# Attention scores in two passes over 128 lines, with queries and keys spread inside SBUF

## The chip, the core and the metric

One NeuronCore of a Trainium2 chip. The metric is the device time of the whole program in microseconds (us), median of several runs. A profile is one more execution, recorded by the hardware; its times are given as us from the start of its span. TensorE is PE in the profile, VectorE is DVE, ScalarE is ACT, GpSimd is POOL, and SyncE, which here only issues transfers, is SP. A "line" of SBUF below is one of its 128 partitions.

## The reference

One layer of a decoder trunk on 512 tokens of width 1024, in float32: an input projection, a causal pooling mixer on 512 channels beside attention on the other 512 (8 heads of 64), an output projection, a gated MLP with a short convolution, and a gated embedding. For 512 tokens in blocks of 256, the selected past blocks and the own block together are plain causal attention, with a bias by distance. What matters here is the scores of a head:

```python
l_own = jnp.einsum('bhqd,bhkd->bhqk', qc, k_own).astype(jnp.float32) * scale + bias_own
l_own = jnp.where(d_own >= 0, l_own, -jnp.inf)
probs = jax.nn.softmax(logits, axis=-1)
```

The contraction is over `d`, the 64 channels of one head.

## The kernel before

**Numbers.** Matmuls run on a 4-byte type (fp32r) that keeps fewer bits than float32. So each operand is held as a pair, a high part `hi` (ACT rounds it) and a low part `lo` (DVE subtracts), and a product is three matmuls into one bank of PSUM: lo by hi, hi by lo, hi by hi (`mm3`, L220 to L222). `split` makes a pair (L225 ACT, L226 DVE).

**Order.** The program writes out the order of each engine's instructions by hand: every engine, and every queue of transfers, takes its instructions in the order of the program text and waits at the first that is not ready. SP issues all transfers of weights.

**Weights.** `_Weights` has a list of chunks of 1 MB. Each lands in one of two buffers `raw` and is split in two steps, each into a pair `wh`, `wl` (ACT L143, DVE L144) that feeds one product. `W.ahead(n)` splits up to n pairs beyond those used. When the second step of a chunk is split, its buffer is free and the chunk after next is issued on SP (L114), which waits for the DVE instruction. In the attention stage chunk 5 is issued in the projection of query pair 0, chunk 6 in that of key pair 0, chunk 7 in the first pooling projection `pool_in(0)`. In `project` these steps come ahead of the rounding of its own result.

**Attention.** `query(hp)` and `key(hp)` project a pair of heads: 24 matmuls of 512 columns into a bank `mm`, then the high part by ACT (L408, or L225) and the low part by DVE (L409, L226), in tiles `qh`, `ql`, `kh`, `kl` with two buffers each. Lines 0 to 63 are the even head, 64 to 127 the odd one. `scores(h)` takes the four query tiles of the causal triangle (128 queries by 512, 384, 128 and 256 keys), three matmuls each on the 64 lines of the head: 12 matmuls. Then DVE adds the bias and finds the maximum (L430), ACT takes the exponential (L432), and DVE normalizes `L` (L433, L436). `transposes(h)` turns `L` into ten 128 by 128 blocks (PE L451), which are split to `PT` (L225, L226). `values(h)` is eight matmuls on `V` and `PT` (L471), low before high at each block of keys.

The loop over heads keeps PE busy with other products (`fills`) while the softmax of a head runs:

```python
    for h in range(H - 1):
        for f in fills[h]:
            f()
        transposes(h)
        scores(h + 1)
        values(h)
```

Ahead of the loop come `query(0)`, `query(1)`, `key(0)`, `key(1)`, the split of `wpool`, and `scores(0)`. `fills` holds the four pooling projections (heads 0, 1, 5, 6), query and key pairs 2 and 3 (heads 2 to 4) and two small products `pool_out` (heads 2 and 3). After the loop the output projection starts, with the transposes and values of head 7 inside it.

Of the kernel before, what the change touches and what calls it, by code (L numbers as in the profile page):

```python
# [17 lines left out]
F32 = mybir.dt.float32  # L18
F32R = mybir.dt.float32r
# [48 lines left out]
class _Weights:  # L68
# [10 lines left out]
    def cols(self, w, col):  # L79

        self.chunks.append(([w[:, col:col + 256].rearrange("(k p) c -> p k c", p=P)], 2))

    def rows(self, w, k0, n, col, width):

        src = w[k0 * P:(k0 + n) * P, col:col + width]
        self.chunks.append(([src.rearrange("(k p) c -> p k c", p=P)], 1))
# [9 lines left out]
    def load(self, between=None):  # L96
        c = self.loaded
        srcs, axis = self.chunks[c]
        self.loaded += 1
        if axis is None:  # L100
            return
        raw = self.pool.tile([P, 2048], F32, tag="raw", name=f"raw{c}", bufs=self.RAW)
        if axis == 0:
            self.raw[c] = raw.rearrange("p (s a b) -> p s a b", s=2, a=2)
            for s, src in enumerate(srcs):
                self.nc.sync.dma_start(self.raw[c][:, s, :src.shape[1], :], src)
        else:
            src = srcs[0]
            self.raw[c] = raw.rearrange("p (a b) -> p a b", a=src.shape[1])
            n = 2 if c < 2 else 1  # L110
            step = src.shape[1] // n
            for i in range(n):
                part = slice(i * step, (i + 1) * step)
                self.nc.sync.dma_start(self.raw[c][:, part, :], src[:, part, :])  # L114
                if between is not None:
                    between(i)

    def ahead(self, n):

        while self.split < min(self.used + n, 2 * len(self.chunks)):  # L120
            c, s = divmod(self.split, 2)
            while self.loaded <= c:
                self.load()
            srcs, axis = self.chunks[c]
            if axis is None:
                view = srcs[s][0]
            elif axis == 0:
                view = self.raw[c][:, s, :srcs[s].shape[1], :]
            else:
                raw = self.raw[c]  # L130
                half = raw.shape[axis] // 2
                part = slice(s * half, (s + 1) * half)
                view = raw[:, part, :] if axis == 1 else raw[:, :, part]
            pair = []
            for kind in "hl":
                t = self.pool.tile([P, 1024], F32R, tag="w" + kind, name=f"w{kind}{self.split}", bufs=self.PAIRS)
                size = view.shape[1] * view.shape[2]
                pair.append(t[:, :size].rearrange("p (a b) -> p a b", a=view.shape[1]))
            if axis is None:
                for t, src in zip(pair, srcs[s]):  # L140
                    self.nc.sync.dma_start(t.bitcast(F32), src)
            else:
                self.nc.scalar.copy(pair[0], view)  # L143
                self.nc.vector.tensor_sub(pair[1], view, pair[0].bitcast(F32))  # L144
            self.pairs[self.split] = pair
            self.split += 1
            if s == 1:
                self.raw.pop(c, None)
                while self.loaded < min(c + 1 + self.RAW, len(self.chunks)):
                    self.load()  # L150
# [8 lines left out]
def hybrid_layer(ctx, tc, x, p, rel_bias, g_mix_pre, g_mix_post, g_ffn_pre, g_ffn_post, w_in, w_pool,  # L159
# [20 lines left out]
    W.cols(w_in, 512)  # L180
    W.cols(w_in, 1024)
    W.cols(w_in, 0)
    W.cols(w_in, 768)
    W.cols(w_in, 1280)
    W.cols(w_in, 256)
    for n in range(2):
        for k0 in (0, 4):
# [36 lines left out]
    def split(pair, src):  # L224
        act.copy(pair[0], src)  # L225
        dve.tensor_sub(pair[1], src, pair[0].bitcast(F32))  # L226
# [173 lines left out]
        W.ahead(n)  # L400
        return ps

    qT, kT, L = {}, {}, {}

    def query(hp):
        ps = project(f"q{hp}")
        hi, lo = qT[hp] = [ap2.tile([P, S], F32R, tag=f"q{c}", name=f"q{c}{hp}", bufs=2) for c in "hl"]
        act.mul(hi, ps, -(DH ** -0.5))  # L408
        dve.scalar_tensor_tensor(lo, ps, -(DH ** -0.5), hi.bitcast(F32), op0=ALU.mult, op1=ALU.subtract)  # L409

    def key(hp):
        ps = project(f"k{hp}")
        kT[hp] = [ap2.tile([P, S], F32R, tag=f"k{c}", name=f"k{c}{hp}", bufs=2) for c in "hl"]
        split(kT[hp], ps)

    place = {3: (0, 0, 768), 2: (1, 0, 384), 0: (1, 384, 0), 1: (2, 0, 128)}

    def scores(h):
        hp, e = divmod(h, 2)
        rows = slice(e * DH, (e + 1) * DH)  # L420
        bk = [bank(f"s{h}_{b}", "s") for b in range(3)]
        for i, (b, c, _) in place.items():
            n = (i + 1) * P
            mm3(bk[b][:, c:c + n], [q[rows, i * P:n] for q in qT[hp]], [q[rows, :n] for q in kT[hp]], True, True)
        L[h] = ap2.tile([P, 1280], F32, tag="L", name=f"L{h}", bufs=1)
        m = small.tile([P, 12], F32, tag="m", name=f"m{h}", bufs=2)
        for i, (b, c, o) in place.items():
            n = (i + 1) * P
            l = L[h][:, o:o + n]
            dve.tensor_tensor_reduce(out=l, in0=bk[b][:, c:c + n], in1=T[:, h, S - n:], scale=1.0, scalar=MASKED,  # L430
                                     op0=ALU.add, op1=ALU.min, accum_out=m[:, i:i + 1])
            act.activation(l, l, AF.Exp, bias=m[:, i:i + 1], scale=-1.0, accum_out=m[:, 4 + i:5 + i])  # L432
        dve.reciprocal(m[:, 8:], m[:, 4:8])  # L433
        for i, (b, c, o) in place.items():
            l = L[h][:, o:o + (i + 1) * P]
            dve.tensor_scalar_mul(l, l, m[:, 8 + i:9 + i])  # L436
# [19 lines left out]
    def moving(q, j):  # L456
        if j < 3:
            o = (P, P + 512, P + 896)[j]
            return q[:, o:o + (NT - j) * P]
        return q.rearrange("p (a b) -> p a b", b=P)[:, 0::10, :]  # L460

    def values(h):
        hp, e = divmod(h, 2)
        ps = bank(f"o{h}", "pt")
        for j in range(NT):
            o = ps[:, min(j, 2) * P:]
            if j == 3:
                o = o.rearrange("p (a b) -> p a b", b=P)
            w = V[:, j, hp, e].rearrange("p a d -> p (a d)")
            for c in (1, 0):  # L470
                pe.matmul(o, w, moving(PT[c], j), start=j == 0 and c == 1, stop=j == NT - 1 and c == 0)  # L471
        rows = slice(e * DH, (e + 1) * DH)
        other = slice((1 - e) * DH, (2 - e) * DH)
        hi, lo = (q[rows, 4 + hp, :] for q in yT)
# [40 lines left out]
    def y_stationary(t, k):  # L515
# [2 lines left out]
    yb = {}  # L518
    part = (4, 5, 0, 1, 6)
    query(0)  # L520
    query(1)
    key(0)
    key(1)
    split(wp, wpool)
    scores(0)
    fills = {0: [lambda: pool_in(0)], 1: [lambda: pool_in(1)],
             2: [lambda: query(2), lambda: pool_out(0)],
             3: [lambda: query(3), lambda: key(2), lambda: pool_out(1)],
             4: [lambda: key(3)], 5: [lambda: pool_in(2)],
             6: [lambda: pool_in(3)]}  # L530
    after = {1: lambda: pool_mid(0), 2: lambda: pool_mid(1), 6: lambda: pool_mid(2)}
    for h in range(H - 1):
        for f in fills[h]:
            f()
        transposes(h)
        scores(h + 1)
        values(h)
        if h in after:
            after[h]()
# [505 lines left out]
```

## Time and profile before

| what | us |
|---|---|
| median of 3 runs | 600.74 (598.84 to 600.99) |
| the profiled execution, its own time | 602.42 |
| its span, first to last instruction | 600.7 |
| PE busy in the span | 591.5 (98%) |
| DVE busy | 429.0 (71%) |
| ACT busy | 293.0 (49%) |
| POOL busy | 235.6 (39%) |

Busy time is read as time in which the engine had an instruction running. PE's is an upper limit of its use, since the ends of matmuls are modelled. 1.7 us of the profiled execution's time lie outside its span. The attention stage runs from about 40 to 145 us: `scores(0)` starts at 61.61 us, the transposes of head 0 at 69.31 and those of head 7 at 145.72.

### The profile page before, as it was taken

What the parts mean: (1) busy time and instruction counts of PE and PEld (TensorE: products, weight loads), DVE (VectorE), ACT (ScalarE), POOL (GpSimd) and SP (SyncE); (2) the same over time, 40 slices, a digit from 0 to 9 for tenths busy, and PEclk for the clock granted to TensorE, in tenths of its full rate; (3) what the DMA queues carried; (4) which work ended last, traced back from release to release, by engine and by line L of the source; (5) the groups of instructions that cost most, each with busy time, mean ns of one, the idle gap of its engine ahead of it and who ended that gap; (6) DMA issues with size and microseconds to landing.
All of it is one profiled execution on the core that took longest, in us unless ns stands there. A gap on an engine that the chain in (4) does not pass through costs nothing.

```text
span 600.7 us, 7462 instructions
## 1 busy us (share of the span) xinstructions
PE 591.5 (98%) x2784; PEld 490.9 (82%) x2784; DVE 429.0 (71%) x556; ACT 293.0 (49%) x476; POOL 235.6 (39%) x236
## 2 busy tenths in 40 slices
PE   9999999999999999999999999999999999999995
PEld 5888888888888998888888888888888788888884
DVE  4653577778378668699855748867778786878984
ACT  5433565575445433344333514625636655765561
POOL 2300230046215559999901697584230000003920
PEclk9999999999999999999999999999999999999999
DMA  8676202122651596999962765867464576852892
GB/s 291 205 269 208 70 1 73 68 71 104 213 167 43 182 361 228 363 335 348 353 210 78 255 210 197 285 237 237 183 214 153 176 280 186 294 189 66 316 308 113
DMA packets 63373, 122.29 MB, mean 204 GB/s; under 512 B 3571, under 2 KB 32847, under 8 KB 61928
## 3 DMA queue, kind: packets, MB, share of 16 engines
q1 hardware_dynamic: 53752, 82.39, 40.8%
q0 software_dynamic: 9584, 39.41, 17.9%
q8 instruction: 22, 0.36, 0.3%
q14 instruction: 15, 0.12, 0.1%
HBM read 97.65 MB, written 26.76 MB: 207 GB/s over the span
## 4 chain that ended last, share of the span: by engine, by line
PE 92%; DVE 2%; DMA 2%; ACT 1%; issue 1%; POOL 0%; SPq 0%; POOLq 0%; DVEq 0%
PE gate L220 6%; PE valu L220 6%; PE valu L222 6%; PE gate L222 6%; PE gate L221 6%; PE valu L221 6%; PE d L220 6%; PE d L222 6%; PE d L221 6%; PE y L220 2%; PE y L221 2%; PE y L222 2%; DMA wl<-gsum 2%; PE g L221 1%; PE o L471 1%; PE g L222 1%
## 5 line engine op out<-in xcount | busy, mean ns | idle before, releaser
L144 DVE TENSOR_TENSOR wl<-raw,wh 128x1024 fp32r<-128x1024 f32 (+1 forms) x118 | 161.5, 1376 | 28.9 <-ACT wh L143 28.4
L143 ACT CAST wh<-raw 128x1024 fp32r<-128x1024 f32 (+1 forms) x118 | 118.8, 1023 | 32.6 <-DMA raw<-in_w_up 13.1
L715 POOL TENSOR_TENSOR b<-b 128x512 f32<-128x512 f32 x60 | 95.8, 1607 | 12.5 <-DMA b<-in_w_down 10.1
L220 PE MATMUL gate<-hT,wl 128*128 128x512 f32 x160 | 62.3, 389 | 0.0
L221 PE MATMUL gate<-hT,wh 128*128 128x512 f32 x160 | 62.3, 389 | 0.0
L222 PE MATMUL gate<-hT,wh 128*128 128x512 f32 x160 | 62.2, 389 | 0.0
L220 PE MATMUL valu<-hT,wl 128*128 128x512 f32 x160 | 62.2, 389 | 0.0
L221 PE MATMUL valu<-hT,wh 128*128 128x512 f32 x160 | 62.2, 389 | 0.0
L222 PE MATMUL valu<-hT,wh 128*128 128x512 f32 x160 | 62.2, 389 | 0.0
L220 PE MATMUL d<-wh,ml 128*128 128x512 f32 x154 | 60.0, 390 | 0.6 <-DVE ml L226 0.6
L222 PE MATMUL d<-wh,mh 128*128 128x512 f32 x154 | 59.9, 389 | 0.0
L221 PE MATMUL d<-wl,mh 128*128 128x512 f32 x154 | 59.9, 389 | 0.0
L250 POOL TENSOR_SCALAR rd<-msd 128x1 f32<-128x1 f32 x4 | 3.2, 798 | 107.1 <-ACT M L245 107.0
L492 POOL TENSOR_TENSOR u<-u 128x512 f32<-128x512 f32 x10 | 11.6, 1158 | 81.7 <-ACT u L488 81.3
L659 ACT ACTIVATE sq<-sq 128x512 f32<-128x512 f32 x22 | 13.9, 633 | 53.8 <-DVE sq L658 53.8
L647 ACT ACTIVATE c<-gate,cols 128x512 f32<-128x512 f32 x20 | 15.5, 773 | 46.9 <-PE gate L222 46.9
L222 PEld LDWEIGHTS gate<-hT,wh 128*128 128x128 f32 x160 | 30.0, 188 | 6.3
L222 PEld LDWEIGHTS valu<-hT,wh 128*128 128x128 f32 x160 | 30.0, 188 | 6.3
L221 PEld LDWEIGHTS valu<-hT,wh 128*128 128x128 f32 x160 | 30.0, 188 | 6.2
L220 PEld LDWEIGHTS valu<-hT,wl 128*128 128x128 f32 x160 | 30.0, 188 | 6.2
L221 PEld LDWEIGHTS gate<-hT,wh 128*128 128x128 f32 x160 | 30.0, 188 | 6.2
L220 PEld LDWEIGHTS gate<-hT,wl 128*128 128x128 f32 x160 | 30.0, 188 | 6.2
(245 smaller groups left out, 1365.0 us busy)
## 6 DMA issues: line engine op xcount, KB each, us to landing
raw<-in_w_up SPq DMA_DIRECT2D x22, 1024.0 KB, 5.3
b<-in_w_down POOLq DMA_DIRECT2D x22, 512.0 KB, 7.4
tsum<-b POOLq DMA_DIRECT2D x11, 1024.0 KB, 5.4
raw<-tsum SPq DMA_DIRECT2D x20, 512.0 KB, 5.6
raw<-in_w_down SPq DMA_DIRECT2D x15, 512.0 KB, 5.9
raw<-in_w_in SPq DMA_DIRECT2D x6, 1024.0 KB, 6.4
raw<-in_w_out SPq DMA_DIRECT2D x4, 1024.0 KB, 5.0
b<-in_w_ple_gate POOLq DMA_DIRECT2D x8, 512.0 KB, 4.6
```

The lines of the kernel that those rows point to most:

```text
L143: self.nc.scalar.copy(pair[0], view)
L144: self.nc.vector.tensor_sub(pair[1], view, pair[0].bitcast(F32))
L220: pe.matmul(o, st[1], mv[0], start=first, stop=False, skip_group_check=more)
L221: pe.matmul(o, st[0], mv[1], start=False, stop=False, skip_group_check=more)
L222: pe.matmul(o, st[0], mv[0], start=False, stop=last, skip_group_check=more)
L250: pool.tensor_scalar(r, ms, add, None, op0=ALU.add)
L471: pe.matmul(o, w, moving(PT[c], j), start=j == 0 and c == 1, stop=j == NT - 1 and c == 0)
L492: pool.tensor_tensor(out=nxt[:, 16:], in0=src[:, 16:], in1=src[:, 16 - (1 << lvl):16 + S - (1 << lvl)], op=ALU.add)
L647: act.activation(c0, pg, AF.Identity, bias=cw[:, 3, f:f + 1], scale=cw[:, 2, f:f + 1])
L659: act.activation(sq, sq, AF.Tanh, scale=GELU_A * GELU_C)
L715: pool.tensor_tensor(out=b[:, o, :], in0=b[:, i0, :], in1=b[:, i1, :], op=ALU.subtract)
```

## The change

The scores take two matmuls over all 128 lines where they took three over 64. For head e of a pair the tile `ST[e][0]` holds the head's `hi` queries on its own 64 lines and the `lo` queries on the other 64. `ST[e][1]` holds the `hi` keys on both halves, and beside them the `lo` keys on both halves. One matmul against the `lo` keys and one against the `hi` keys then sum all four products (the low by low one too, which was left out). The pair's result is first written to one tile `QK` (query high, key high, key low, query low; one buffer) and from there copied to `ST` by transfers within SBUF, issued on SP: four of 128 KB for the queries of a pair, four of 256 KB for its keys. `QK` and `ST` have one buffer each, so the next pair's query or key can be written to `QK` only when the transfers have read it, and the next pair's transfers may write `ST` only when the scores have read it.

The order of the weights is changed to match (chunks 5 and 6 each hold a query pair and a key pair in rows of 512 bytes, in two transfers, where they held two query pairs or two key pairs in rows of 1 KB), and query 3 comes behind key 2. `values` takes all its high parts first, then the low ones.

```diff
+    def two(self, w, *cols):
+        self.chunks.append(([w[:, c:c + P].rearrange("(k p) c -> p k c", p=P) for c in cols], 3))
...
-    W.cols(w_in, 768)
-    W.cols(w_in, 1280)
+    for c in (768, 896):
+        W.two(w_in, c, c + 512)
...
+    QK = ap2.tile([P, 4, S], F32R, name="qk")
+    ST = [[ap2.tile([P, S], F32R, name=f"q_{e}"), ap2.tile([P, 2, S], F32R, name=f"k_{e}")] for e in range(2)]

     def query(hp):
         ps = project(f"q{hp}")
-        hi, lo = qT[hp] = [ap2.tile([P, S], F32R, tag=f"q{c}", name=f"q{c}{hp}", bufs=2) for c in "hl"]
-        act.mul(hi, ps, -(DH ** -0.5))
-        dve.scalar_tensor_tensor(lo, ps, -(DH ** -0.5), hi.bitcast(F32), op0=ALU.mult, op1=ALU.subtract)
+        act.mul(QK[:, 0, :], ps, -(DH ** -0.5))
+        dve.scalar_tensor_tensor(QK[:, 3, :], ps, -(DH ** -0.5), QK[:, 0, :].bitcast(F32), op0=ALU.mult,
+                                 op1=ALU.subtract)

     def key(hp):
         ps = project(f"k{hp}")
-        kT[hp] = [ap2.tile([P, S], F32R, tag=f"k{c}", name=f"k{c}{hp}", bufs=2) for c in "hl"]
-        split(kT[hp], ps)
+        split([QK[:, 1, :], QK[:, 2, :]], ps)
+
+    def spread_queries():
+        for e in range(2):
+            for a in range(2):
+                sp.dma_start(ST[e][0][a * DH:(a + 1) * DH].bitcast(F32),
+                             QK[e * DH:(e + 1) * DH, 0 if a == e else 3, :].bitcast(F32))
+
+    def spread_keys():
+        for e in range(2):
+            for a in range(2):
+                sp.dma_start(ST[e][1][a * DH:(a + 1) * DH].bitcast(F32), QK[e * DH:(e + 1) * DH, 1:3, :].bitcast(F32))

     def scores(h):
-        hp, e = divmod(h, 2)
-        rows = slice(e * DH, (e + 1) * DH)
+        q, k = ST[h % 2]
...
-            mm3(bk[b][:, c:c + n], [q[rows, i * P:n] for q in qT[hp]], [q[rows, :n] for q in kT[hp]], True, True)
+            for a in (1, 0):
+                pe.matmul(bk[b][:, c:c + n], q[:, i * P:n], k[:, a, :n], start=a == 1, stop=a == 0)
...
     def values(h):
-        for j in range(NT):
...
-            for c in (1, 0):
-                pe.matmul(o, w, moving(PT[c], j), start=j == 0 and c == 1, stop=j == NT - 1 and c == 0)
+        for c in range(2):
+            for j in range(NT):
...
+                pe.matmul(o, w, moving(PT[c], j), start=j == 0 and c == 0, stop=j == NT - 1 and c == 1)
...
     query(0)
+    spread_queries()
     query(1)
     key(0)
+    spread_keys()
     key(1)
     split(wp, wpool)
     scores(0)
...
-             3: [lambda: query(3), lambda: key(2), lambda: pool_out(1)],
+             3: [lambda: key(2), spread_keys, lambda: query(3), lambda: pool_out(1)],
...
         scores(h + 1)
+        if h in (0, 2, 4):
+            spread_queries()
+            if h != 2:
+                spread_keys()
         values(h)
```

## Rows read from the trace of the kernel before

**Rows 1.** The page of the kernel before: the chain of work that ended last, by engine.

```profile
PE 92%; DVE 2%; DMA 2%; ACT 1%; issue 1%; POOL 0%; SPq 0%; POOLq 0%; DVEq 0%
```

**Rows 2.** The waits of TensorE (PE) over the whole span, the one of the attention stage: who waited <- for whom, us in total, times, longest.

```profile
PE pt L451 <- DVE L L436: 0.5, 1, 0.5
```

**Rows 3.** Timeline of PE from the transposes of head 0 to the end of the projection behind `values(0)`: start us, us, line, operation, what it writes <- reads, x how many. An instruction's own length is modelled and overlaps the next, so the pace is the distance of two starts.

```profile
69.31 1.25 PE L451 MATMUL pt<-ident,L 128*128 128x128 f32 x10
70.50 0.50 PE L220 MATMUL s<-kh,ql 64*128 64x512 f32 x1
...
71.30 0.33 PE L220 MATMUL s<-kh,ql 64*128 64x384 f32 x1
71.47 0.34 PE L221 MATMUL s<-kl,qh 64*128 64x384 f32 x1
...
71.89 0.27 PE L221 MATMUL s<-kl,qh 64*128 64x128 f32 x1
72.00 0.27 PE L222 MATMUL s<-kh,qh 64*128 64x128 f32 x1
...
72.61 1.56 PE L471 MATMUL o<-PT,V 128*128 128x512 f32 x8
74.01 0.40 PE L220 MATMUL u<-hT,wl 128*128 128x512 f32 x1
...
79.23 0.39 PE L222 MATMUL u<-hT,wh 128*128 128x512 f32 x1
```

**Rows 4.** The same view at three places without 64-line matmuls beside them: the transposes and `values` of head 7, and a run of 38 matmuls of 256 columns.

```profile
145.72 1.29 PE L451 MATMUL pt<-ident,L 128*128 128x128 f32 x10 [0.47 <-DVE L L436]
146.76 0.48 PE L220 MATMUL y<-wh,yT 128*128 128x512 f32 x1
...
150.99 1.44 PE L471 MATMUL o<-PT,V 128*128 128x512 f32 x8
152.27 0.40 PE L220 MATMUL y<-wh,yT 128*128 128x512 f32 x1
...
203.54 0.28 PE L222 MATMUL up<-hT,wh 128*128 128x256 f32 x1
...
207.98 0.28 PE L220 MATMUL up<-hT,wl 128*128 128x256 f32 x1
```

**Rows 5.** Busy time by stretch, from one head's transposes to the next one's (heads 1 and 5): us from:to, length, then busy us (instructions) of PE, weight load, DVE, ACT, POOL, then PE's granted clock, DMA share, GB/s.

```profile
79.46:90.27 10.81, 10.81 (x58) 9.16 (x57) 7.92 (x20) 7.35 (x17) 5.03 (x5) 1.00 0.00 0
...
126.82:136.95 10.13, 10.13 (x55) 8.60 (x54) 7.36 (x19) 7.30 (x16) 6.06 (x6) 1.00 0.30 104
```

**Rows 6.** Timeline of VectorE (DVE): the low halves of the transposed probabilities (L226, three each) of heads 1 and 2, and the last normalization before the transposes of head 7.

```profile
80.84 1.62 DVE L226 TENSOR_TENSOR PT<-pt,PT 128x512 fp32r<-128x512 f32 x3 [1.65 <-ACT PT L225]
...
91.86 1.61 DVE L226 TENSOR_TENSOR PT<-pt,PT 128x512 fp32r<-128x512 f32 x3
...
143.80 1.90 DVE L436 TENSOR_SCALAR L<-L,m 128x512 f32<-128x512 f32 x4
```

**Rows 7.** Timeline of ScalarE (ACT): the high halves of query pair 1 and, two projections later, of key pair 1.

```profile
50.84 0.60 ACT L408 ACTIVATE qh<-q 128x512 fp32r<-128x512 f32 x1 [3.90 <-PE q L222]
...
61.71 0.59 ACT L225 CAST kh<-k 128x512 fp32r<-128x512 f32 x1 [3.90 <-PE k L222]
```

**Rows 8.** Timeline of DVE: the low half of query pair 0, and the normalization of head 0.

```profile
46.03 0.69 DVE L409 SCALAR_TENSOR_TENSOR ql<-q,qh 128x512 fp32r<-128x512 f32 x1 [1.09 <-ACT qh L408]
...
66.81 1.27 DVE L436 TENSOR_SCALAR L<-L,m 128x512 f32<-128x512 f32 x4
```

**Rows 9.** Issues on the queue of SyncE (SPq) of chunks 3, 5, 6 and 7 of the weights, 1 MB each: start us, us that the issue took.

```profile
17.31 0.40 SPq L114 DMA_DIRECT2D raw<-in_w_in  x1
...
44.96 0.37 SPq L114 DMA_DIRECT2D raw<-in_w_in  x1
...
53.66 0.37 SPq L114 DMA_DIRECT2D raw<-in_w_in  x1
...
69.24 0.37 SPq L114 DMA_DIRECT2D raw<-in_w_in  x1
```

**Rows 10.** GB/s of all transfers in 40 equal slices of a window: 20 to 25 us, 44 to 55 us, and 53 to 60 us.

```profile
GB/s 385 393 385 385 393 385 385 385 393 393 377 369 381 320 291 66 0 0 0 0 0 0 0 0 0 0 0 0 0 0 0 0 0 0 0 0 131 124 126 2
...
GB/s 387 402 432 432 387 357 447 328 402 402 343 432 358 305 376 335 339 350 354 350 361 346 346 298 123 93 0 0 0 0 0 0 0 0 0 0 0 0 11 141
...
GB/s 0 0 0 0 0 0 0 0 0 23 129 222 129 64 146 181 316 374 386 410 386 380 380 392 380 380 386 374 363 187 47 0 0 0 0 0 0 0 0 0
```

**Rows 11.** DMA: issues, KB each and median us from issue to landing, of chunk 3 (issued in 17 to 18 us) and of two tiles of x (issued in 4.05 to 6 us); the packets, MB and share of 16 engines of SyncE's queue in 75 to 100 us (one chunk in rows of 2 KB) and in 60 to 75 us (one in rows of 1 KB); and all transfers of 25 to 32 us, where a copy within HBM (`scr` from `line`) runs alone.

```profile
raw<-in_w_in SPq DMA_DIRECT2D x1, 1024.0 KB, 5.2
...
xa<-in_x SPq DMA_DIRECT2D x2, 512.0 KB, 10.4
...
q1 hardware_dynamic: 528, 1.05, 12.2%
...
q1 hardware_dynamic: 1040, 1.05, 22.1%
...
DMA packets 695, 1.38 MB, mean 197 GB/s; under 512 B 427, under 2 KB 427, under 8 KB 695
```

**Rows 12.** Timeline of PE at the program's opening.

```profile
12.75 0.63 PE L221 MATMUL v<-wl,hT 128*128 128x512 f32 x1
13.18 0.63 PE L222 MATMUL v<-wh,hT 128*128 128x512 f32 x1
```

More of the change, by code (lines that the diff above doesn't have):

```diff
@@ L102, in load @@
         raw = self.pool.tile([P, 2048], F32, tag="raw", name=f"raw{c}", bufs=self.RAW)
-        if axis == 0:
-            self.raw[c] = raw.rearrange("p (s a b) -> p s a b", s=2, a=2)
+        if axis in (0, 3):
+            self.raw[c] = raw.rearrange("p (s a b) -> p s a b", s=2, a=2 if axis == 0 else 8)
             for s, src in enumerate(srcs):
@@ L126, in ahead @@
                 view = srcs[s][0]
-            elif axis == 0:
+            elif axis in (0, 3):
                 view = self.raw[c][:, s, :srcs[s].shape[1], :]
@@ L401, in project @@
         return ps
-    qT, kT, L = {}, {}, {}
+    L = {}
+    QK = ap2.tile([P, 4, S], F32R, name="qk")
+    ST = [[ap2.tile([P, S], F32R, name=f"q_{e}"), ap2.tile([P, 2, S], F32R, name=f"k_{e}")] for e in range(2)]
     def query(hp):
         ps = project(f"q{hp}")
-        hi, lo = qT[hp] = [ap2.tile([P, S], F32R, tag=f"q{c}", name=f"q{c}{hp}", bufs=2) for c in "hl"]
-        act.mul(hi, ps, -(DH ** -0.5))
-        dve.scalar_tensor_tensor(lo, ps, -(DH ** -0.5), hi.bitcast(F32), op0=ALU.mult, op1=ALU.subtract)
+        act.mul(QK[:, 0, :], ps, -(DH ** -0.5))
+        dve.scalar_tensor_tensor(QK[:, 3, :], ps, -(DH ** -0.5), QK[:, 0, :].bitcast(F32), op0=ALU.mult,
+                                 op1=ALU.subtract)
     def key(hp):
         ps = project(f"k{hp}")
-        kT[hp] = [ap2.tile([P, S], F32R, tag=f"k{c}", name=f"k{c}{hp}", bufs=2) for c in "hl"]
-        split(kT[hp], ps)
+        split([QK[:, 1, :], QK[:, 2, :]], ps)
[8 more added lines that the diff above has]
+                sp.dma_start(ST[e][1][a * DH:(a + 1) * DH].bitcast(F32), QK[e * DH:(e + 1) * DH, 1:3, :].bitcast(F32))
     place = {3: (0, 0, 768), 2: (1, 0, 384), 0: (1, 384, 0), 1: (2, 0, 128)}
     def scores(h):
-        hp, e = divmod(h, 2)
-        rows = slice(e * DH, (e + 1) * DH)
+        q, k = ST[h % 2]
         bk = [bank(f"s{h}_{b}", "s") for b in range(3)]
@@ L464, in values @@
         ps = bank(f"o{h}", "pt")
-        for j in range(NT):
[L466 to L469, printed above, removed]
-            for c in (1, 0):
-                pe.matmul(o, w, moving(PT[c], j), start=j == 0 and c == 1, stop=j == NT - 1 and c == 0)
+        for c in range(2):
+            for j in range(NT):
+                o = ps[:, min(j, 2) * P:]
+                if j == 3:
+                    o = o.rearrange("p (a b) -> p a b", b=P)
+                w = V[:, j, hp, e].rearrange("p a d -> p (a d)")
+                pe.matmul(o, w, moving(PT[c], j), start=j == 0 and c == 0, stop=j == NT - 1 and c == 1)
         rows = slice(e * DH, (e + 1) * DH)
```

## The prediction

> **What bounds the kernel now.** The chain of work that ended last is 92% PE [rows 1], so first the list of PE's waits is read: in the attention stage PE waits once, for 0.5 us, at the transposes of head 7 [rows 2]. Up to there PE goes without a pause. What is taken from PE between 40 and 127 us comes off the end, as long as the engines that feed it keep up. The second view is the timeline of PE around one head, for the price of scores on 64 lines [rows 3] beside the same work without them [rows 4]. The third is the timelines of ACT and DVE, which show how late each is against PE [rows 6 to 8]. The fourth is the queue of transfers, since the change puts new ones into it [rows 9 to 11].
>
> **What two passes give.** From the transposes of head 0 to the product behind its values there are 74.01 - 69.31 = 4.70 us: 1.19 up to the first score, 2.11 for the scores, 1.40 for the values [rows 3]. In head 7, where no 64-line matmul stands beside them, transposes take 1.04 and values 1.28 [rows 4]; so the turn into 64 lines and back costs 0.27. The scores become eight matmuls on 128 lines. At that shape 512 columns go every (79.23 - 74.01)/23 = 0.227 us [rows 3] and 256 every (207.98 - 203.54)/37 = 0.120 [rows 4]; for 384 and 128 I take the 64-line pace, 0.17 to 0.18 and 0.11 [rows 3]. Two of each: 1.27. So a head falls from 4.70 to 1.04 + 1.27 + 1.28 = 3.59, by 1.11 us. By columns alone it would be a third of the matmuls' time, 0.7. The Trainium skill (TensorEngine Tiling (Array Packing), Key Properties) says that changing the tiling mode drains the engine; the trace agrees, with the 0.27 above.
>
> Five such heads, with `scores(1)` to `scores(5)`, lie between the transposes of head 0 (call it T0, 69.31 [rows 3]) and those of head 5 (126.82 [rows 5]): **-5.55 us**. From there to the transposes of head 7 the gain stops. DVE ends the normalization for them at 143.80 + 1.90 = 145.70, and they start at 145.72 [rows 4, 6]: these 18.9 us go by DVE and ACT, whose instructions stay. `scores(6)` and `scores(7)` give nothing.
>
> **What DVE takes back.** From the low halves of head 1 to those of head 2 DVE takes 91.86 - 80.84 = 11.02 us [rows 6], about 10.8 without a short wait for query 2. PE's stretch of 10.81 [rows 5] falls to 9.7. So the low halves of head 2 begin 2.5 us after its transposes, where those of head 1 began 80.84 - 79.46 = 1.4 after, and end 1.6 later, at 4.1. `values(2)` starts at 1.04 + 1.27 = 2.3; with high parts first it wants the last low ones at 3.3: **+0.8 us**. The new order of `values` has no other effect: elsewhere it hides, behind 0.64 us of high parts, that the scores now end earlier.
>
> **What the transfers cost.** `QK` has one buffer. So ACT must not write query 1 until all four transfers of query 0 have read it, nor key 1 until those of key 0 have. SP's queue is kept in order: the last two x tiles, issued behind some 3 MB, landed 10.4 us after issue [rows 11].
>
> Query 0 is ready at 46.7 [rows 8], but chunk 5 was issued at 44.96 [rows 9] and its packets run to the 26th slice of its window, 51.15 [rows 10]. In rows of 512 bytes it takes longer: a packet of 2 KB takes 0.122 x 25 x 16 / 528 = 92 ns, one of 1 KB 51 [rows 11], so one of 512 bytes about 30, and 1 MB in 2048 of them 3.9 us instead of 3.3: +0.6, to 51.75.
>
> No row shows a copy inside SBUF, so 512 KB (four query transfers, or two key transfers) are bounded. Fast: 256 packets of 2 KB at 92 ns on 16 engines, 1.5 us. Slow: the copy within HBM, 197 GB/s [rows 11], 2.7 us. I take 2.0, nearer to the rows with SBUF at one end. A landing comes 0.5 us behind the last packet (chunk 3: 17.31 + 5.2 = 22.5, packets to 22.0 [rows 9 to 11]). Then step by step, with 1.5 / 2.0 / 2.7:
>
> - Queries land at 53.75 / 54.25 / 54.95. ACT stands at query 1, which began at 50.84 [rows 7], until then; behind it waits weight pair 9, and SP waits for that pair's DVE step before it issues chunk 6.
> - Chunk 6 is issued 53.66 - 50.84 = 2.82 after query 1 [rows 7, 9], at 56.6 / 57.1 / 57.8. Its packets ended at 58.43 [rows 10], 4.8 after issue; with 0.6 for the short rows, at 62.0 / 62.5 / 63.2.
> - The keys of pair 0, ready near 58, queue behind it. Those of head 0 land at 64.0 / 65.0 / 66.4, all at 65.5 / 67.0 / 69.1. `scores(0)` was due at 61.6: PE idles 2.4 / 3.4 / 4.8 us.
> - ACT can write key 1 only now, not at 61.71 [rows 7]. Behind it on ACT and DVE stand the split of `wpool` and the whole softmax of head 0, which ended 6.4 us after it (66.81 + 1.27 = 68.1 [rows 8]). So T0 is 71.9 / 73.4 / 75.5, later than 69.31 by **2.6 / 4.1 / 6.2 us**. PE itself, with 1.27 of scores and 5.45 of projection, would be there 1.2 / 1.7 / 2.4 earlier.
>
> Pair 1: chunk 7 is issued 69.24 - 68.1 = 1.2 after T0 [rows 8, 9] and its packets end at T0 + 6.0. Behind it come all queries and head 2's keys, 1 MB, landing at T0 + 9.5 / 10.5 / 11.9; `scores(2)` wants them at T0 + 9.04 + 1.04 = 10.1. The wait, 0 / 0.4 / 1.8, overlaps the 0.8 at `values(2)`: together 0.8 / 0.8 / 1.8. Pairs 2 and 3 have no chunk ahead of them and land 0.1 to 2 us early, so I take nothing. SP's eight issues at some 0.4 us [rows 9] run beside this; only weights stand behind them, with a head's time to spare.
>
> **Sum.** -5.55 + 4.1 + 0.8 = -0.65 us, with bounds -2.15 and +2.45. After head 7 PE is the chain again, so the difference is carried to the end. The profiled execution took 602.42, 1.7 above the median; -0.65 there is 601.8, and on the median 600.74 it is **600.1 us**.
>
> **Rivals.**
>
> *The queue does not hold the copies up* (0.24). If they pass chunks 5 and 6 or share the engines with them, ACT and key 1 are on time, and T0 is PE's own, about 1.0 early by `scores(0)`: -1.0 - 5.55 + 0.8 = -5.75, 595.0. For it: the engines' GB/s are zero from 51.2 to 54.5 [rows 10], so room is near. Against: the x tiles' 10.4 us [rows 11]. It decides (below 597.7) when T0 comes before 71.0.
>
> *Copies at 200 GB/s or less* (0.18). Each touches 64 lines at either end, which no row here shows. At the slow bound the sum is +2.45, 603.2. It would show at `scores(2)`, which then waits 1.8. The Trainium skill (SBUF — State Buffer, Door 1: The DMA port swizzle) states that lines 0 to 63 reach only half of the 16 ports, with 196 GB/s measured for 1 MiB; by that 512 KB take 2.7 us, an estimate from the page. No run here shows it yet.
>
> *The clock falls in PE's pause* (0.13), the case on the slower side. PE idles 2.4 to 4.8 us at `scores(0)`, as it does nowhere between its opening and the end of attention. At the opening 512 columns take 13.18 - 12.75 = 0.43 us [rows 12], the pace of 1.2 GHz, against 0.227. If `scores(0)` and the first pooling projection run at that pace, their 1.27 and 24 matmuls take 1.3 + 4.8 = 6.1 us more; 1.7 hides behind the softmax, and 4.4 are left: 604.5, or 606.9 with slow copies. The kernel is slower by 0.5% once 5.4 of the 6.1 are lost, with copies at my middle value.
>
> *Two passes cost as much as three* (0.03): then 604 to 605; the 128-line pace speaks against it.
>
> **The numbers.** My forecast with its own range, 598.6 to 602, has 0.42. Half a per cent, 3.0 us, is what a measurement of this kernel can tell from no change: faster is below 597.7, slower above 603.7. Faster takes the first rival and a tail of the forecast, 0.27; slower the clock, the last rival and a tail of the slow copies, 0.16; the rest is 0.57. The range runs from 596, inside the first rival, to 604, inside the clock's.
>
> **What would show it.** Two passes: from transposes to the product behind `values`, 3.6 us a head and eight score matmuls at the paces above. The queue: ACT's query 1 at 54 instead of 50.84, chunk 6 issued at 57, PE waiting some 3.4 us at `scores(0)`, the transposes of head 0 near 73. The DVE limit: transposes of heads 5 and 7 still 18.9 apart. I am wrong if ACT writes query 1 before 52, if more than one later score waits for a copy, or if PE's pace halves behind its pause.

## The result, and the profile after

The changed kernel takes 605.62 us in the median (605.41 to 606.21, 4 runs), the kernel before 599.84 in the runs beside it (598.84 to 600.99). The ratio is 1.0097, with a 95% interval of 1.0072 to 1.0122: slower by one per cent, and 1.6 us above the upper end of the forecast range.

The profiled execution of the changed kernel took 605.41 us with a span of 603.6. Its PE row names the places at once: it falls to 6 in the fifth slice, where PEclk falls to 7, and to 8 in the tenth. The page of the changed kernel, TensorE and its clock in 40 slices:

```profile
PE   9999699998999999999999999999999999999996
...
PEclk9999799998999999999999999999999999999999
```

A slice is 15.1 us, so these are 60 to 75 and 136 to 151 us. The waits of PE from 30 to 155 us in the changed kernel; before, one wait of 0.5 stood here [rows 2]:

```profile
PE s L444 <- issue: 5.0, 2, 4.7
PE o L491 <- DVE PT L230: 2.1, 1, 2.1
PE k L224 <- DVE qk L416: 0.4, 1, 0.4
```

The first line is `scores(0)` (4.7) and `scores(2)` (0.36), both waiting for copies. The view calls it "issue" where it has no releaser for a wait; at `scores(0)` in two of the kernels below it names the key copies (`DMA k<-qk`). ACT, in the same execution, says what was late, at query 1 and key 1 [rows 7]:

```profile
45.56 0.60 ACT L415 ACTIVATE qk<-q 128x512 fp32r<-128x512 f32 x1 [1.97 <-PE q L226]
...
55.34 0.60 ACT L415 ACTIVATE qk<-q 128x512 fp32r<-128x512 f32 x1 [8.25 <-DMA q<-qk]
...
69.29 0.59 ACT L229 CAST qk<-k 128x512 fp32r<-128x512 f32 x1 [10.98 <-DMA k<-qk]
```

Query 1 was rounded 4.5 us later than before (50.84), key 1 7.6 later (61.71), each after a wait for the copies that still read `QK`. SP's queue shows the link between the two [rows 9]: chunk 6, in rows of 512 bytes, is issued at 58.16 instead of 53.66, and the keys behind it.

```profile
45.06 0.99 SPq L110 DMA_DIRECT2D raw<-in_w_in  x2
46.18 4.51 SPq L427 DMA_DIRECT2D q<-qk  x4
58.16 1.00 SPq L110 DMA_DIRECT2D raw<-in_w_in  x2
59.27 4.39 SPq L434 DMA_DIRECT2D k<-qk  x4
```

What was moved, in GB/s, in 40 slices of 44 to 56 us (0.3 us each: chunk 5, then the queries) and of 57 to 70 us (0.325 each: chunk 6, then the keys) [rows 10]:

```profile
GB/s 410 423 423 396 355 410 396 410 355 369 410 394 295 273 311 311 290 294 312 304 297 297 295 297 309 275 253 246 294 253 191 89 41 14 14 20 0 0 0 0
...
GB/s 0 0 0 0 0 0 9 95 33 210 339 350 348 328 307 293 298 284 321 391 202 126 139 240 252 227 227 214 227 227 240 252 177 88 13 0 0 0 0 0
```

The short rows run at about 297 (before 350, [rows 10]). The packets of chunk 6 are through by 63.4; from there to 68.1 the keys go at 207 GB/s in the mean, 0.97 MB, and at 214 to 252 in the middle. In the first window the bulk ends at about 53.4, a thin tail of 14 to 41 runs on to 54.8, and the landing comes 0.5 behind that.

Then PE. `scores(0)`, the first product behind the pause, and where its pace changes [rows 3, 12]:

```profile
67.16 2.68 PE L444 MATMUL s<-k,q 128*128 128x512 f32 x8 [4.67 <-issue]
69.64 0.63 PE L224 MATMUL u<-hT,wl 128*128 128x512 f32 x1
70.07 0.63 PE L225 MATMUL u<-hT,wh 128*128 128x512 f32 x1
...
72.63 0.44 PE L225 MATMUL u<-hT,wh 128*128 128x512 f32 x1
72.91 0.39 PE L226 MATMUL u<-hT,wh 128*128 128x512 f32 x1
73.14 0.39 PE L224 MATMUL u<-hT,wl 128*128 128x512 f32 x1
```

For 5.5 us after the pause 512 columns take 0.43 us, the pace of the opening [rows 12], and the granted clock of 66.9 to 72.8 is 0.51, which is 1.2 GHz. Then the pace is 0.23 again. Head 0 itself, from its transposes to the projection behind `values(0)`:

```profile
76.56 1.25 PE L471 MATMUL pt<-ident,L 128*128 128x128 f32 x10
77.57 1.53 PE L444 MATMUL s<-k,q 128*128 128x512 f32 x8
78.94 1.46 PE L491 MATMUL o<-PT,V 128*128 128x512 f32 x8
80.23 0.40 PE L224 MATMUL u<-hT,wl 128*128 128x512 f32 x1
```

1.01 + 1.37 + 1.29 = 3.67 us where it was 4.70 [rows 3]: the two passes give what they should. Last the stretch between the transposes of heads 5 and 7, in the timelines of DVE and POOL [rows 6]:

```profile
139.94 3.21 DVE L148 TENSOR_TENSOR wl<-raw,wh 128x1024 fp32r<-128x1024 f32 x2
143.18 1.62 DVE L230 TENSOR_TENSOR PT<-pt,PT 128x512 fp32r<-128x512 f32 x3
147.99 2.46 DVE L456 TENSOR_SCALAR L<-L,m 128x512 f32<-128x512 f32 x4
...
140.23 6.29 POOL L512 TENSOR_TENSOR u<-u 128x512 f32<-128x512 f32 x4 [2.84 <-ACT u L508]
```

Before, the normalization took 1.90 [rows 6]. The two splits took 2.36 and were nearly over when POOL's four additions began (the same timelines, kernel before):

```profile
136.60 2.36 DVE L144 TENSOR_TENSOR wl<-raw,wh 128x1024 fp32r<-128x1024 f32 x2
...
137.89 5.58 POOL L492 TENSOR_TENSOR u<-u 128x512 f32<-128x512 f32 x4 [3.84 <-ACT u L488]
```

**The account.** All kernels below were read at the starts of the transposes: T0 of head 0, T5 of head 5, T7 of head 7, counted from the rounding of query 0 (R), since the opening of the program differs by up to 2 us from one execution to another (R is at 45.40 before, 45.56 after, 43.55 in one run below).

| kernel | R to T0 | T0 to T5 | T5 to T7 | R to T7 | median us |
|---|---|---|---|---|---|
| before | 23.91 | 57.51 | 18.90 | 100.32 | 599.84 |
| after | 31.00 | 53.60 | 20.17 | 104.77 | 605.62 |

So +7.1 up to T0, -3.9 in the five heads, +1.3 behind them: +4.45 us. The medians differ by 5.8, with an interval of 4.3 to 7.3. Behind T7 the kernels are alike: 453.3 to the end of the span after, and 453.2 to 453.8 in the ten kernels below. The 455.0 of the profiled execution before holds 1.4 of a late landing at its own end, which is why the two spans differ by 2.9 only.

### The profile page after: what moved, and what is told of

Read it like the earlier page. It is cut to its first block, busy times and chain, and to the rows that moved or that the text cites. A ratio compares the mean times of both kernels' runs of the same rounds, so it can differ in the third digit from the quotient of the medians.

```text
span 603.6 us, 7483 instructions
## 1 busy us (share of the span) xinstructions
PE 588.9 (98%) x2752; PEld 489.5 (81%) x2752; DVE 424.0 (70%) x556; ACT 292.6 (48%) x476; POOL 234.8 (39%) x236
## 4 chain that ended last, share of the span: by engine, by line
PE 92%; DVE 2%; DMA 2%; ACT 1%; issue 1%; SPq 0%; POOL 0%; DVEq 0%; ACTq 0%; POOLq 0%
PE gate L224 6%; PE valu L224 6%; PE gate L226 6%; PE valu L226 6%; PE gate L225 6%; PE valu L225 6%; PE d L224 6%; PE d L226 5%; PE d L225 5%; PE y L226 2%; PE y L224 2%; PE y L225 2%; PE g L226 2%; PE g L225 2%; PE g L224 2%; PE o L491 2%
## 5 line engine op out<-in xcount | busy, mean ns | idle before, releaser
L148 DVE TENSOR_TENSOR wl<-raw,wh 128x1024 fp32r<-128x1024 f32 (+1 forms) x118 | 156.9, 1336 | 23.1 <-ACT wh L147 22.6
L226 PE MATMUL gate<-hT,wh 128*128 128x512 f32 x160 | 62.2, 389 | 0.0
L226 PE MATMUL valu<-hT,wh 128*128 128x512 f32 x160 | 62.2, 389 | 0.0
L226 PE MATMUL d<-wh,mh 128*128 128x512 f32 x154 | 59.9, 389 | 0.0
L674 DVE SCALAR_TENSOR_TENSOR c<-gate,cols,c 128x511 f32<-128x511 f32 x20 | 14.9, 745 | 29.7 <-ACT c L673 29.7
L226 PEld LDWEIGHTS gate<-hT,wh 128*128 128x128 f32 x160 | 30.0, 188 | 6.3
L226 PEld LDWEIGHTS valu<-hT,wh 128*128 128x128 f32 x160 | 30.0, 188 | 6.3
```

The costliest lines, as they stand in the source:

```text
L226: pe.matmul(o, st[0], mv[0], start=False, stop=last, skip_group_check=more)
L674: dve.scalar_tensor_tensor(c0[:, 1:], pg[:, :S - 1], cw[:, 1, f:f + 1], c0[:, 1:], op0=ALU.mult, op1=ALU.add)
```

## The experiments

### The parts one at a time

Three kernels take the change apart. In the first the kernel before makes two passes over 128 lines straight on its own tiles, without a copy; it leaves the low queries out and sums both heads of a pair.

```diff
-            mm3(bk[b][:, c:c + n], [q[rows, i * P:n] for q in qT[hp]], [q[rows, :n] for q in kT[hp]], True, True)
+            for a in (1, 0):
+                pe.matmul(bk[b][:, c:c + n], qT[hp][0][:, i * P:n], kT[hp][a][:, :n], start=a == 1, stop=a == 0)
```

> The kernel before with two passes over 128 lines straight on its query and key tiles, without any copy: it leaves out the low parts of the queries and mixes the two heads of a pair, so it only shows what the passes give. Theory A: 1.0 us a head up to head 5, transposes of head 0 near 68.3, of head 7 near 140, 594 to 595.5 us, 5 to 6 below the kernel before. Theory B (VectorE gives nothing back): less than 3 us below before, 597 us or more.

Measured: 596.24 us (595.42 to 596.49), ratio 0.9941 [0.9927, 0.9956]. The two passes alone are worth 3.6 us, less than the 5 to 6 of theory A. T0 to T5 is 53.80, T5 to T7 20.18 where it was 18.90. So the 1.3 us lost behind head 5 come with the two passes and not with the copies.

The second has the changed kernel's copies but three matmuls on 64 lines (the high by high product stands twice, high queries by low keys once, and low queries not at all):

```diff
-            for a in (1, 0):
-                pe.matmul(bk[b][:, c:c + n], q[:, i * P:n], k[:, a, :n], start=a == 1, stop=a == 0)
+            e = h % 2
+            own = slice(e * DH, (e + 1) * DH)
+            o = bk[b][:, c:c + n]
+            pe.matmul(o, q[own, i * P:n], k[own, 0, :n], start=True, stop=False)
+            pe.matmul(o, q[own, i * P:n], k[own, 1, :n], start=False, stop=False)
+            pe.matmul(o, q[own, i * P:n], k[own, 0, :n], start=False, stop=True)
```

> The changed kernel with all its copies, but three matmuls on the head's 64 lines of the copied tiles (high by high twice in place of low by high), so that only the passes are undone. Theory A: the start as in the changed kernel, transposes of head 0 at 77 to 78, and 1 us a head lost behind it: about 610 us. If the passes give nothing in this schedule: 605 to 606 us.

Measured: 607.62 us (606.60 to 608.02), ratio 1.0131 [1.0116, 1.0146], 2.0 above the changed kernel and not the 4.4 expected. T0 to T5 is 57.83, within 0.3 of before, and T5 to T7 is 18.91 again, the figure of before to 0.01. Of the 4.2 us that three passes lose in the heads they get 1.3 back behind them and 0.3 ahead of them; the traces then differ by 2.7, the medians by 2.0. Both kernels with short heads so far have 20.2 behind head 5, and both with long ones 18.9.

The third is the kernel before with the new order of weights (chunks in rows of 512 bytes), key 2 ahead of query 3 and the new order of `values`:

```diff
-    W.cols(w_in, 768)
-    W.cols(w_in, 1280)
+    for c in (768, 896):
+        W.two(w_in, c, c + 512)
...
-             3: [lambda: query(3), lambda: key(2), lambda: pool_out(1)],
+             3: [lambda: key(2), lambda: query(3), lambda: pool_out(1)],
```

> The kernel before with the parts of the change that are no passes and no copies: weight chunks 5 and 6 in rows of 512 bytes, key 2 ahead of query 3, and values with all high parts first. Every theory: no wait becomes longer, same as before within 0.3%, 598 to 601.5 us; slower by over 1 us would put a part of the loss on the weights' rows.

Measured: 599.81 us (598.78 to 600.78, 10 runs), ratio 1.0001 [0.9992, 1.0011]. No change, as expected; T0 to T5 is 57.58 and T5 to T7 18.48.

### The wait for the copies

If the single `QK` and late copies are the cause, it is enough to ask for `QK` later. In the next kernel the order ahead of the loop is query 0, key 0, query 1, key 1, so that a projection lies between a copy and the write that waits for it.

```diff
-    W.cols(w_in, 512)
-    W.cols(w_in, 1024)
+    for c in (512, 640):
+        W.two(w_in, c, c + 512)
...
     query(0)
     spread_queries()
-    query(1)
     key(0)
     spread_keys()
+    query(1)
     key(1)
```

> Projects query 0, key 0, query 1, key 1 in this order (weight chunks 2 and 3 hold a query pair and a key pair each), so that pair 0's copies have two projections to land in. Theory A (the loss is pair 0's copies on the path at the start): no wait of PE at the first scores, transposes of head 0 near 68.5 us instead of 76.56, and the whole about 8 us shorter than the changed kernel, 597 to 599 us, some 2 us below the kernel before. Theory B (the loss is spread over the stage, by contention of the copies and by VectorE): at most 2 us shorter, 603 to 605 us.

Measured: 597.77 us (597.30 to 598.46), ratio 0.9965 [0.9953, 0.9976]: 7.9 below the changed kernel, and faster than the kernel before. `scores(0)` starts at 61.61 as before, T0 is 68.34, and the pause is gone. Its waits of PE from 30 to 150 us:

```profile
PE o L491 <- DVE PT L230: 2.1, 1, 2.1
PE s L444 <- DMA k<-qk: 1.4, 1, 1.4
```

This settles the place, but not what holds the copies. A second buffer for `QK` was not tried.

The prediction said SP's queue, which is kept in order. The next kernel takes pair 0's copies out of it:

```diff
-    def spread_queries():
+    def spread_queries(sp=sp):
...
-    def spread_keys():
+    def spread_keys(sp=sp):
...
-    spread_queries()
+    spread_queries(pool)
...
-    spread_keys()
+    spread_keys(pool)
```

> The changed kernel with one edit: pair 0's copies are issued from POOL's queue in place of SP's, so that they don't stand in one queue with weight chunks 5 to 7. Theory that the copies and the weight chunks lose time by the order of SP's queue: query 1 is there at 51 to 53 us in place of 55.3, chunk 6 is issued by 56 in place of 58.2, key 1 is there at 63 to 67 in place of 69.3, and the whole is 1.5 to 3 us shorter than the changed kernel's 605.6 (602.5 to 604.0). Rival, that the copies are slow by themselves and the queue is of no account: query 1 again at about 55, key 1 at about 69, the whole 605 to 606.

Measured: 605.39 us (605.08 to 605.60), ratio 1.0092 [1.0067, 1.0118]. That is the rival's number. POOL issued the four query copies within 2.3 us, and they landed no earlier:

```profile
45.56 0.54 POOL L427 DMA_DIRECT2D q<-qk  x1 [4.48 <-ACT qk L415]
46.29 1.55 POOL L427 DMA_DIRECT2D q<-qk  x3 [0.18 <-issue]
...
55.25 0.60 ACT L415 ACTIVATE qk<-q 128x512 fp32r<-128x512 f32 x1 [9.05 <-DMA q<-qk]
```

So SP's queue is not it. What changed is when chunk 5 lands: the time from issue to landing, in KB each and median us, of its two transfers and of the queries, in the changed kernel and then here.

```profile
raw<-in_w_in SPq DMA_DIRECT2D x2, 512.0 KB, 5.7
q<-qk SPq DMA_DIRECT2D x4, 128.0 KB, 5.5
...
raw<-in_w_in SPq DMA_DIRECT2D x2, 512.0 KB, 7.8
q<-qk POOLq DMA_DIRECT2D x4, 128.0 KB, 7.8
```

With the copies on another queue they and the chunk share the engines: the chunk lands 2.1 us later, and the last copy no earlier. The Trainium skill (DMA: Bandwidth & Descriptors, Issuing engines are not separate DMA queues) has the rule: whatever engine starts a transfer, all run on the same 16 engines and interleave there, and a second starting engine only saves the time of the issues. The trace agrees, with query 1 at 55.25 and 55.34. For the queries POOL's queue was not free either, since the 2 MB of the bias table `T`, issued on it at 40.13, landed 8.9 us later. For the keys it was free, and there too the first packets came only as those of chunk 6 ended, at about 63. Either the copies are slow by themselves, or the chunk issued just before holds them, whatever queue they come from. The next kernel issues chunks 5 and 6 behind the copies; neither is needed before T0.

```diff
+    hold = False
...
-                while self.loaded < min(c + 1 + self.RAW, len(self.chunks)):
-                    self.load()
+                self.done = c
+                if not self.hold:
+                    self.fetch()
+
+    def fetch(self):
+        while self.loaded < min(self.done + 1 + self.RAW, len(self.chunks)):
+            self.load()
...
+    W.hold = True
     query(0)
     spread_queries()
+    W.fetch()
     query(1)
     key(0)
     spread_keys()
+    W.fetch()
+    W.hold = False
     key(1)
```

> The changed kernel with the two weight chunks that are in flight beside pair 0's copies (5 and 6) issued behind them instead of ahead of them; both are needed only after the transposes of head 0. Run g1 has shown that SP's queue isn't what holds the copies. Theory that the chunk's packets hold them, since both share the 16 engines: with nothing ahead, query 1 is there at 51 to 52.5 us in place of 55.3 and key 1 at 62.5 to 65 in place of 69.3, the transposes of head 0 start at 69.5 to 72, and the whole is 4 to 6 us shorter than the changed kernel (599.5 to 601.5). Rival, that the copies themselves take the 8 to 10 us from issue to landing: query 1 at 54 or later, key 1 at 67 or later, the whole 603.5 or more.

Measured: 599.87 us (598.77 to 600.50, 10 runs), ratio 0.9995 [0.9983, 1.0007], 5.7 below the changed kernel. The theory of the chunk's packets holds. ACT and the transfers of 56 to 70 us (0.35 us a slice) in this execution, whose R is 2.0 earlier than after's:

```profile
52.21 0.60 ACT L421 ACTIVATE qk<-q 128x512 fp32r<-128x512 f32 x1 [7.12 <-DMA q<-qk]
...
62.71 0.59 ACT L235 CAST qk<-k 128x512 fp32r<-128x512 f32 x1 [6.81 <-DMA k<-qk]
```

```profile
GB/s 0 0 187 199 187 187 199 187 187 187 304 328 222 222 238 186 151 205 325 303 293 291 310 310 306 300 184 40 0 0 0 0 0 0 0 0 0 0 0 0
```

From R to key 1 it takes 19.2 us instead of 23.7, and 25.3 to T0 instead of 31.0. There is no halved pace any more; the pause at `scores(0)` is 0.5. The first eight slices in which anything moves are key copies with nothing beside them, at 187 to 199 GB/s.

Counted from R, query 1 gains only 1.1 us (8.7 instead of 9.8). But R is no fixed point for the transfers: the engines still carry the table `T` when the queries are issued, and `T` is issued at 40.57 here and at 40.02 in the changed kernel. Counted from there query 1 comes after 11.6 us instead of 15.3. T0, at 68.87, lies below the expected 69.5 to 72 because R is 2.0 earlier.

### The clock

To tell the clock's share in T0 from that of the wait, PE was given work in the pause: 48 transposes into a bank of its own ahead of `scores(0)`.

```diff
     split(wp, wpool)
+    fill = bank("fill", "pt")
+    for _ in range(48):
+        pe.transpose(fill[:, :P], ident, ident)
     scores(0)
```

> The changed kernel with 48 transposes of the identity (about 5 us) ahead of the first scores, into a bank that nobody reads, so that PE is not idle in its pause. Theory A with the clock as a part of the loss: the matmuls behind the pause keep the pace of 2.4 GHz, the transposes of head 0 come 6.4 us after key 1 instead of 7.3, and the whole is about 0.9 us shorter (604.7). If the clock costs nothing, because the softmax is awaited anyway: same as the changed kernel within 0.3 us.

Measured: 608.58 us (605.32 to 611.27), ratio 1.0147 [1.0108, 1.0186]; not shorter at all. PE in that execution:

```profile
62.59 5.40 PE L549 MATMUL fill<-ident 128*128 128x128 f32 x48
67.74 1.53 PE L444 MATMUL s<-k,q 128*128 128x512 f32 x8
69.11 0.39 PE L224 MATMUL u<-hT,wl 128*128 128x512 f32 x1
69.34 0.40 PE L225 MATMUL u<-hT,wh 128*128 128x512 f32 x1
...
75.73 1.46 PE L471 MATMUL pt<-ident,L 128*128 128x128 f32 x10 [0.97 <-DVE L L456]
...
90.90 1.51 PE L444 MATMUL s<-k,q 128*128 128x512 f32 x3 [4.57 <-DMA k<-qk]
```

For T0 it answers the question. The pace stays at 0.23, T0 comes 6.2 us after key 1 (69.56) instead of 7.3, and PE waits 0.97 for DVE there. So the clock's share is 1.1 in that execution of the changed kernel, and DVE limits what more can be had. It is not the same in every execution. With the copies on POOL's queue PE paused as long:

```profile
66.93 2.25 PE L444 MATMUL s<-k,q 128*128 128x512 f32 x8 [4.57 <-issue]
...
70.69 0.48 PE L225 MATMUL u<-hT,wh 128*128 128x512 f32 x1
...
75.33 1.33 PE L471 MATMUL pt<-ident,L 128*128 128x128 f32 x10
```

There the granted clock was still 1.00 up to the scores and 0.54 from 69 to 71 us, the slow pace was over at 70.69, and T0 came 6.3 after key 1 (69.04). With three passes PE paused for 2.9 and six matmuls behind the scores were slow, and T0 came 6.2 after key 1. So the clock cost 1.1 us once and about 0.1 or nothing in two other executions.

The last row of the kernel with the filled pause is another matter: pair 1's key copies were late in its execution, with transfers nearly still from 87 to 89 us and SP's four key issues taking 7.24 us instead of 3.42. The spread of its times, 6 us, suggests that this comes and goes. Why the copies stalled is left open.

### Going on from the pair order

Two more edits on top of the reordered kernel. In the first one weight pair more is split ahead in query 3, key 3 and `pool_in(2)`, so that one split, not two, stands on DVE between heads 5 and 6:

```diff
-        ps = project(f"q{hp}")
+        ps = project(f"q{hp}", n=4 if hp == 3 else 3)
...
-        ps = project(f"k{hp}")
+        ps = project(f"k{hp}", n=4 if hp == 3 else 3)
...
-        ps = project(f"u{g}", n=4 if g == 3 else 3)
+        ps = project(f"u{g}", n=4 if g >= 2 else 3)
```

> e1 with one weight split moved from head 6 up to the long stretch of head 3 (n=4 for query 3, key 3 and pooling projection 2). Theory: the 1.3 us that every kernel with two passes loses between the transposes of heads 5 and 7 (20.2 instead of 18.9) are VectorE's two weight splits beside GpSimd's pooling; with one split fewer the stretch falls to 18.7 or below and the whole by 1.3 to 1.6 us, to 596.3. Rival: the stretch is set by the softmax alone and stays at 20.2; same as e1.

Measured: 595.45 us (595.30 to 595.76), ratio 0.9938 [0.9923, 0.9953], where it was 0.9965 without the edit, so 1.6 us less. T5 to T7 is 17.92 in place of 20.21, and the wait at `values(6)` is gone. DVE and POOL in this execution:

```profile
131.87 1.23 DVE L148 TENSOR_TENSOR wl<-raw,wh 128x1024 fp32r<-128x1024 f32 x1
133.54 1.62 DVE L230 TENSOR_TENSOR PT<-pt,PT 128x512 fp32r<-128x512 f32 x3 [0.45 <-ACT PT L229]
138.34 1.64 DVE L456 TENSOR_SCALAR L<-L,m 128x512 f32<-128x512 f32 x4
...
133.10 4.65 POOL L512 TENSOR_TENSOR u<-u 128x512 f32<-128x512 f32 x4 [3.78 <-ACT u L508]
```

In the second the even head's copies of the next pair are issued a head earlier, as soon as its own scores have read `ST`:

```diff
     scores(0)
+    spread_queries((0,))
+    spread_keys((0,))
...
-             2: [lambda: query(2), lambda: pool_out(0)],
+             2: [lambda: query(2), lambda: spread_queries((0,)), lambda: pool_out(0)],
...
-             4: [lambda: key(3)], 5: [lambda: pool_in(2)],
+             4: [lambda: key(3), lambda: spread_keys((0,))], 5: [lambda: pool_in(2)],
...
-            spread_queries()
+            spread_queries((1,))
             if h != 2:
-                spread_keys()
+                spread_keys((1,))
+        if h == 3:
+            spread_queries((0,))
```

> e1 with the copies of a pair's even head issued as soon as the scores of the even head before have read its tile, ahead of those of the odd head. Theory: the wait of 1.35 us at the scores of head 2 in e1 is late landing; it goes, and the stretch from the transposes of head 1 to those of head 2 falls from 11.4 to 10.0: 596.4 us. Rival: VectorE is late there by 0.8 anyway, so only 0.5 us come back: 597.3.

Measured: 597.25 us (595.87 to 598.56), ratio 0.9966 [0.9954, 0.9978], and 0.9965 for the kernel it starts from: no gain that the times show, where the two intervals would leave room for up to 1 us. The wait of 1.4 at `scores(2)` is gone from the trace, and the stretch from head 1's transposes to head 2's falls from 11.42 to 10.26. But T0 to T7 falls by 1.0 only (74.69 to 73.69). Both together:

> e1 with both of these. If they are separate losses: the sum, 594.5 to 595.5 us, the level of the kernel with two passes and no copies (596.2) or a little below it, since that one has the 1.3 us too.

Measured: 594.30 us (593.41 to 595.61), ratio 0.9920 [0.9903, 0.9936]: the best of all, 5.0 us below the kernel before in the same rounds (599.27), and by the two ratios 1.8% below the changed kernel. PE waits 1.0 us in all from 30 to 150 us:

```profile
PE pt L471 <- DVE L L456: 0.8, 2, 0.6
PE mix L225 <- DVE p L230: 0.2, 1, 0.2
```

## Why the prediction was wrong

The sum was -5.55 + 4.1 + 0.8 = -0.65 us. From R to T7 the traces give +7.1 - 3.9 + 1.3 = +4.45. The step that failed is the term for the transfers, +4.1 with bounds of 2.6 and 6.2: T0 came 7.1 us later. The path was the right one (late copies, one `QK`, late key 1), but landing, copy rate and clock on it were each put too low. A second step failed beside it: the 0 between T5 and T7 was +1.3. Term by term:

- **Two passes, -5.55, with +0.8 for DVE: mostly right.** A head costs 3.67, forecast 3.59; the difference is the scores, 1.37 for 1.27. Over five heads the change is -3.91 where -4.75 was forecast. The 0.8 at `values(2)` did not come as such: there is a wait of 0.36 at `scores(2)` and one of 0.4 at the key behind it. Rival "two passes cost as much as three" is out, by the 3.6 us of the kernel without copies.
- **The transfers, +4.1: the right mechanism, too small.** Queries were to land at 54.25 and were there at 55.34 (+1.1): the copies' bulk ended at about 53.4, near the 53.75 of the forecast, but the last packets trickled on to 54.8, and "a landing comes 0.5 us behind the last packet" was taken from a weight chunk that has no such tail. Chunk 6 followed query 1 by 2.82 us, exactly as in the kernel before. Key 1 came 11.1 after that issue instead of 9.9 (+1.2): counted from the issue, the keys' bulk ended 0.5 later than forecast, at 68.05, and landed 1.2 behind that and not 0.5. T0 followed key 1 by 7.3 instead of 6.4 (+0.9), in this execution by the clock. 4.1 + 1.1 + 1.2 + 0.9 = 7.3, against +7.25 in the times of the two traces.
- **"SP's queue is kept in order"** was the reason given, and it is not what costs the time. On a queue of their own the copies land at the same time; with the chunks behind them they land early enough to save 5.7 us. The rival that the queue does not hold the copies up was right in its name and wrong in its time. It had query 1 and key 1 on time if the copies passed the chunks or shared the engines with them. On POOL's queue the queries did share, and chunk 5 landed 7.8 us after its issue in place of 5.7, but the last of them was no earlier for it.
- **The clock (a rival, 0.13) did fall**, and on top of the forecast, not in its place. Its price was 4.4 us and turned out as 1.1 at most: it held down the scores and seven of the 24 matmuls behind them, 2.5 us in all, where all 24 were priced, and most of it hid behind the softmax. A halved pace behind the pause was one of the prediction's own signs of being wrong. The pause itself was in the forecast (3.4 us; it was 4.7), and no row of before showed PE after a pause of 3 us within its steady work, so 0.13 rested on no row.
- **"From there the gain stops"** (0 between T5 and T7) was a loss of 1.3. The stretch was read as DVE's and ACT's with unchanged instructions. Their number is unchanged, but not their length: with PE's heads shorter, DVE's two splits fall into POOL's additions. They take 3.21 in place of 2.36, the normalization 2.46 in place of 1.90: 1.4 together. That this loss belongs to the shorter heads is shown, by 20.18 without copies and 18.91 with copies and three passes. That POOL's additions are what slows DVE is how the rows read, and was not isolated; the run with a split moved fits it. The Trainium skill (SBUF — State Buffer, Who interferes with whom) has a rule for it that the prediction did not weigh: a DVE instruction with two inputs in SBUF, as the split is, contends with a GpSimd instruction that reads SBUF. The 3.21 agrees with it.
- **The copies' rate, 2.0 us for 512 KB**, was too fast: from 63.4 on the keys went at 207 GB/s, 2.5 us for 512 KB and near the slow bound of 2.7. That is the 0.5 by which their bulk was late. The rival of slow copies was near the rate, but not the time: its price at that bound was +2.45, and its sign, 1.8 us at `scores(2)`, was 0.36.

The bounds of +4.1 (2.6 to 6.2) moved the copies' rate and nothing else. Landing tails, rate and clock all erred to one side, and 7.1 lay outside.

## What to carry to other kernels

A copy that a later write must wait for is to be placed by what is in flight on the DMA engines when it starts, not by its own size or its queue: issue it ahead of bulk that nobody needs yet, or put another piece of work between it and the waiting write, as the order by pairs did for 7.9 us. A wait can be paid more than once: the chunk behind the waiting instruction delayed the next copies, and behind the pause PE ran at half its clock, which cost up to 1.1 us more. And work that PE saves shifts what runs beside what; before counting on unchanged instructions of another engine, look at what they will now overlap.

## What the runs showed of the hardware

- Copies inside SBUF between halves of the lines: keys alone, 187 to 199 GB/s; behind a chunk, 207 in the mean and 214 to 252 in the middle. The Trainium skill (SBUF — State Buffer, Door 1: The DMA port swizzle) measured 196 for lines 0 to 63 at 1 MiB; the trace agrees where the copies run alone, and is above it where they follow a chunk, which was not taken apart.
- A queue of their own did not bring copies past bulk that was already under way. The query copies, behind chunk 5, had `QK` free at 55.34 us from SP's queue and at 55.25 from POOL's, 15.3 and 15.1 us after the issue of the table `T`; ahead of the chunk it took 11.6. Even ahead of it ACT waited 7 us, with 380 to 430 GB/s beside them at first, which is mostly `T`. On one queue chunk 5 landed 5.7 us after its issue, with the copies on the other 7.8: there the two shared the engines. Key copies on POOL's queue, issued from 58.93 on, moved only as chunk 6 ended, at about 63.
- The time that issues take on SP varies: the four query copies took 4.51 us behind chunk 5 and 2.49 ahead of it. The engines moved some 400 GB/s at the start of both, so a busy engine alone does not explain it; what does was not tried.
- After 4.7 us of idle PE the granted clock was 0.51, which is 1.2 GHz, and the slow pace lasted for 5.5 us; after 4.6 in another execution it ended 3.8 us behind the start of the scores. A pause filled with transposes left the clock at 1.00, which is 2.4 GHz, from 62 to 76 us. After the 2.1 us wait at `values(6)` the pace also halved, in the profiled executions of the changed kernel and three others, and not in three more with the same wait; there DVE set T7 in any case. At the opening the slow pace [rows 12] stands beside a granted clock that the profile gives as 1.00, so there the pace alone shows it.
- The opening of the program took up to 2 us more or less from one execution to the next, with nothing changed in it: R is at 45.56 in the changed kernel, 43.57 with the filled pause.
